# The first layer's FFN by seven block products as well, with its weight sums formed by POOL inside the stage

## The chip, the cores and the metric

The kernel runs on one core of a Trainium2 chip. The metric is the time of one execution on the device in microseconds (us); of the kernel before, three runs gave a median of 1687.15 us (1685.29 to 1689.51). The five engines of the core work beside each other: TensorE (PE) multiplies matrices, VectorE (DVE), ScalarE (ACT) and GpSimd (POOL) work on elements, SyncE (SP) starts the transfers (DMA). Each engine takes its instructions from its own queue in order and waits on semaphores for the others.

## The reference

Two layers over 512 latent tokens and 256 context tokens with 1024 features. Each layer mixes tokens by four groups of heads, and then applies a gated FFN with 2816 hidden features; shifts, scales and gates of each come from a conditioning vector by a matrix `w_mod`:

```python
def swiglu(h, w_in_, w_out_):
    gate, up = jnp.split(h @ w_in_, 2, axis=-1)
    return (jax.nn.silu(gate) * up) @ w_out_
...
    sh_a, sc_a, g_a, sh_f, sc_f, g_f = jnp.split((jax.nn.silu(c) @ w_mod + b_mod)[:, None, :], 6, axis=-1)
...
    x = x + g_a * rms_norm(mix_x @ w_out, norm_g[1])
    x = x + g_f * rms_norm(swiglu(modulate(rms_norm(x, norm_g[2]), sh_f, sc_f), w_ffn_in, w_ffn_out), norm_g[3])
```

`modulate(h, shift, scale)` is `h * (1 + scale) + shift`. All is float32. The output is the latent tokens after both layers.

## The kernel before

**Arithmetic.** Activations lie with features on the 128 partitions and tokens along the free axis. A float32 product is made of three matmuls: `split` (line 411) takes an operand apart into a rounded high part by ACT (`wh`, line 416) and the rest by DVE or POOL (`wl`, line 417), and `mac3` (line 489, matmuls on lines 491 to 493) multiplies high by high, high by low and low by high.

**FFN, plain.** The hidden features are 22 tiles of 128. For each, `ffn` loads two weight units of 512 KB (gate and up) into a ring of raw tiles `wr`, splits them, multiplies 8 blocks of features for each of gate and up, and gates. So a plain tile is 2 x 8 x 3 = 48 matmuls of 512 columns. Tiles are taken in chunks (`fcx`: 0 to 7, 8 to 14, 15 to 21), and behind each chunk the down product adds its hidden tiles to eight outputs `y`. The first three tiles and, of the last chunk, six of the eight outputs are done for the first 256 tokens and then for the second 256 (`halved`), so that the norm of one half runs beside matmuls of the other: behind the first half `ends` and `residual` norm it, and `then` starts the next layer's norm.

**FFN by seven block products.** Layer 1 uses `ffn_seven` and `strassen_pair`. Gate and up of one tile, the two halves of the features and the two halves of the tokens form a 2 by 2 block product, done by seven block products in place of eight; each is 4 x 3 = 12 matmuls of 256 columns, 84 per tile. It needs sums of blocks of the activations (`strassen_rhs`, once, `sx` and `st` tiles) and of the weights (`form_sums`, four 128 x 512 operations per tile). The first chunk's tiles stay plain, while these are formed. The weights' sums are either formed at the tile's turn, two operations by POOL and two by DVE (`sad`), or beforehand: `weight_sums` queues a task per tile that loads the two units, forms the sums by POOL alone (line 1566) and stores them, 1 MB, in DRAM (`ws`); the tile then loads them.

**Where the tasks run.** `tick` is called whenever a weight unit is fetched, and adds a rate to a counter; at 1 it takes one task off a queue. There are two queues: `bg` holds the tasks of the modulation (`mods_sums`: 32 tasks for layer 1, each one load of 512 KB and two multiply-adds by DVE into `macc`, lines 696 and 698; the totals go through PE on line 704 and DVE on line 708 to `mod`), and `bg2` the weights' sums. During layer 0's FFN `bg` runs at 0.2 per tick, and what is left is done by `flush` in `then`, at the boundary between the layers; `bg2` makes the sums of layer 1's nine even tiles 4 to 20 at 0.17 per tick.

**Order.** The program text gives priorities (`urgent` marks the norm chains as early); a scheduler with a time model then fixes each engine's queue before the run. Rings decide when buffers come free: raw weights `wr` for units, `wq` for the down weights of chunks, PSUM tiles `mm` and `mx`.

## Time and profile before

| | |
|---|---|
| median of three runs | 1687.15 us |
| profiled execution | 1681.38 us, span 1679.6 us |
| PE busy | 1596.8 us, 95% of the span |
| DVE, ACT, POOL busy | 1062.5, 792.8, 761.4 us |
| mean DMA rate | 146 GB/s |
| layer 0's FFN | about 640 to 1050 us of the span |
| boundary to layer 1 | about 1015 to 1060 us |
| layer 1's mixer | about 1053 to 1306 us |
| layer 1's FFN | about 1306 to 1680 us |

A time of the profile is counted from the start of the span. A busy engine is not an engine that works at its peak: matmuls overlap, so their pace is read from their starts and not from their durations. PEclk is the clock that TensorE was granted, where 1.00 is 2.4 GHz and 0.50 is 1.2 GHz. Idle time of an engine is listed with what ended it; for an engine that nothing waits for it costs nothing.

### The profile page before, as it was taken

The page shows a single profiled execution, that of the slowest core. Times are in us where ns is not written, and L with a number is a line of the kernel's source. Part 1 is how long each engine was busy: PE and PEld are TensorE (multiplying, and loading weights), DVE is VectorE, ACT ScalarE, POOL GpSimd, SP SyncE. Part 2 cuts the span into 40 slices and gives each one's busy share as a digit, 9 for nine tenths or more (in the row PEclk, how much of TensorE's full clock was granted, in tenths as well). Part 3 has the DMA queues.
Part 4 walks back from the last instruction along what each step waited for, and adds up shares of the span by engine and source line. Part 5 has one row for each costly group of instructions (what it writes and reads, how often), then busy time and mean ns, then how long its engine had stood idle before and what let it go on. Part 6 is the DMA issues. An engine that isn't in the chain of part 4 may idle for free.

```text
span 1679.6 us, 29082 instructions
## 1 busy us (share of the span) xinstructions
PE 1596.8 (95%) x10616; PEld 1395.7 (83%) x10616; DVE 1062.5 (63%) x2312; ACT 792.8 (47%) x1782; POOL 761.4 (45%) x797
## 2 busy tenths in 40 slices
PE   6999998998999998999999997999699999999997
PEld 2976877887899897888888887999569989999996
DVE  4887676648785668532343478658774866665664
ACT  3665356654445555332332333565374545555451
POOL 2431235554466565444335324332424665564653
PEclk8999998999999999999999998999799999999998
DMA  9854563354475323445545676131031224444441
GB/s 325 271 190 160 179 201 101 123 176 142 126 247 176 117 80 124 153 155 199 180 158 171 209 249 225 40 96 64 26 93 59 95 88 132 133 138 131 126 127 58
DMA packets 94734, 245.37 MB, mean 146 GB/s; under 512 B 12032, under 2 KB 21120, under 8 KB 94592
## 3 DMA queue, kind: packets, MB, share of 16 engines
q1 hardware_dynamic: 94592, 243.52, 44.2%
q8 instruction: 83, 1.36, 0.3%
q14 instruction: 59, 0.48, 0.1%
HBM read 227.76 MB, written 15.73 MB: 145 GB/s over the span
## 4 chain that ended last, share of the span: by engine, by line
PE 64%; DVE 7%; issue 1%; DMA 1%; POOL 1%; ACT 1%; DVEq 0%; POOLq 0%; SPq 0%; ACTq 0%
PE mm L491 16%; PE mm L493 15%; PE mm L492 15%; PE mx L493 2%; PE mx L491 2%; PE mx L492 2%; PE mm L508 1%; PE mm L513 1%; PE mm L514 1%; PE mm L515 1%; PE mm L509 1%; DVE wl L417 1%; PE mm L520 1%; PE mx L1420 1%; PE mx L1168 1%
## 5 line engine op out<-in xcount | busy, mean ns | idle before, releaser
L417 POOL TENSOR_TENSOR wl<-wr,wh 128x512 fp32r<-128x512 f32 (+2 forms) x268 | 358.9, 1344 | 428.1 <-ACT wh L416 390.5
L416 ACT ACTIVATE wh<-wr 128x512 fp32r<-128x512 f32 (+3 forms) x548 | 334.9, 619 | 459.3 <-PE mm L492 340.0
L417 DVE TENSOR_TENSOR wl<-wr,wh 128x512 fp32r<-128x512 f32 (+3 forms) x280 | 220.5, 790 | 155.1 <-ACT wh L416 149.7
L491 PE MATMUL mm<-hfh_m,wh 128*128 128x512 f32 (+1 forms) x320 | 124.6, 389 | 0.0
L493 PE MATMUL mm<-hfh_m,wl 128*128 128x512 f32 (+1 forms) x320 | 124.3, 388 | 0.0
L492 PE MATMUL mm<-hfl_m,wh 128*128 128x512 f32 (+1 forms) x320 | 123.9, 387 | 0.0
L492 PE MATMUL mm<-hfl_c,wh 128*128 128x256 f32 x352 | 100.3, 285 | 0.6 <-POOL hfl_c L603 0.6
L491 PE MATMUL mm<-hfh_c,wh 128*128 128x256 f32 x352 | 100.6, 287 | 0.0
L493 PE MATMUL mm<-hfh_c,wl 128*128 128x256 f32 x352 | 99.4, 283 | 0.0
L491 PEld LDWEIGHTS mm<-hfh_c,wh 128*128 128x128 f32 x352 | 66.1, 188 | 6.6 <-issue 2.7
L493 PEld LDWEIGHTS mm<-hfh_m,wl 128*128 128x128 f32 x320 | 60.1, 188 | 13.5
L492 PEld LDWEIGHTS mm<-hfl_m,wh 128*128 128x128 f32 x320 | 60.1, 188 | 13.2
L491 PEld LDWEIGHTS mm<-hfh_m,wh 128*128 128x128 f32 x320 | 60.1, 188 | 12.9
L492 PEld LDWEIGHTS mm<-hfl_c,wh 128*128 128x128 f32 x352 | 66.4, 189 | 2.4 <-issue 1.0
L493 PEld LDWEIGHTS mm<-hfh_c,wl 128*128 128x128 f32 x352 | 66.4, 189 | 0.8 <-issue 0.4
L492 PE MATMUL mm<-gl_m,wh 128*128 128x512 f32 x152 | 59.7, 394 | 0.0
L493 PE MATMUL mm<-gh_m,wl 128*128 128x512 f32 x152 | 59.7, 394 | 0.0
L491 PE MATMUL mm<-gh_m,wh 128*128 128x512 f32 x152 | 59.6, 394 | 0.0
L698 DVE SCALAR_TENSOR_TENSOR macc_m<-wr,cs,macc_m 128x512 f32<-128x512 f32 x56 | 45.8, 836 | 18.0 <-DMA wr<-in_wmod_dram 17.6
L1566 POOL TENSOR_TENSOR wr<-wr,wr 128x512 f32<-128x512 f32 x36 | 52.8, 1479 | 1.1
L491 PE MATMUL mx<-gh_m,wh 128*128 128x512 f32 x128 | 50.9, 399 | 1.4 <-ACT wh L416 1.4
L493 PE MATMUL mx<-gh_m,wl 128*128 128x512 f32 x128 | 51.2, 400 | 1.0 <-POOL wl L417 0.6
(721 smaller groups left out, 5329.2 us busy)
## 6 DMA issues: line engine op xcount, KB each, us to landing
wr<-in_wfi_dram SPq DMA_DIRECT2D x141, 512.0 KB, 3.6
wr<-in_wmod_dram SPq DMA_DIRECT2D x80, 512.0 KB, 4.4
wr<-in_wT_dram SPq DMA_DIRECT2D x42, 512.0 KB, 4.4
wr<-in_wo_dram SPq DMA_DIRECT2D x24, 512.0 KB, 4.2
wr<-in_wfo_dram SPq DMA_DIRECT2D x24, 512.0 KB, 4.0
wr<-ws SPq DMA_DIRECT2D x18, 512.0 KB, 3.9
wm_m<-in_wmod_dram SPq DMA_DIRECT2D x32, 256.0 KB, 5.3
wr<-in_wfo_dram SPq DMA_DIRECT2D x16, 448.0 KB, 3.9
```

What stands on the lines that cost most here:

```text
L416: nc.scalar.activation(hi, src, AF.Copy)
L417: (eng or nc.vector).tensor_tensor(out=lo, in0=src, in1=hi.bitcast(F32), op=ALU.subtract)
L491: nc.tensor.matmul(out, lh, rh, start=first, stop=False, skip_group_check=more)
L492: nc.tensor.matmul(out, lh, rl, start=False, stop=False, skip_group_check=more)
L493: nc.tensor.matmul(out, ll, rh, start=False, stop=last, skip_group_check=more)
L508: nc.tensor.matmul(out, w.h[w0 + i], ah, start=f, stop=False)
L509: nc.tensor.matmul(out, w.l[w0 + i], ah, start=False, stop=False)
L513: nc.tensor.matmul(out[:, c], w.h[w0 + i], ah[:, c], start=f and q == 0, stop=False)
L514: nc.tensor.matmul(out[:, c], w.h[w0 + i], al[:, c], start=False, stop=False)
L515: nc.tensor.matmul(out[:, c], w.l[w0 + i], ah[:, c], start=False, stop=z and q == 1)
L698: nc.vector.scalar_tensor_tensor(out=t, in0=w, scalar=self.cs[:, k, s:s + 1], in1=t, op0=ALU.mult, op1=ALU.add)
L1566: tt = lambda i, o, a, b, op=ALU.subtract: self.e(engines[i]).tensor_tensor(out=o, in0=a, in1=b, op=op)
```

## The change

Layer 0's FFN is done by `ffn_seven` too. Its first chunk are six plain tiles (0 to 5), then come four chunks of four tiles by block products. Eight of its sixteen tiles (7, 9, ... 21) get their weights' sums from tasks that POOL works off during the stage itself, at 0.5 per tick; a task whose tile was already formed at its turn is skipped (`formed`). The modulation's tasks of layer 1 run at 0.5 per tick. Layer 1's nine sums tasks move to layer 1's mixer, at 0.3 per tick, with the rest at its end. The down weights of a first chunk of over five tiles come through `wr` and not through `wq`.

```diff
- 'strassen': (1,),
- 'fcs': ((0, 4), (4, 7), (7, 11), (11, 16), (16, 22)),
- 'sums0': tuple(range(4, 22)),
+ 'strassen': (0, 1),
+ 'fcs0': ((0, 6), (6, 10), (10, 14), (14, 18), (18, 22)),
+ 'fcs1': ((0, 4), (4, 7), (7, 11), (11, 16), (16, 22)),
+ 'sums0': tuple(range(7, 22, 2)),
...
- 'pre_l0': 0.35,
- 'pre_f0': 0.17,
+ 'pre_f0': 0.5,
...
-        self.bg2.extend(lambda j=j: task(j) for j in js)
+        self.bg2.extend(lambda j=j: (l, j) in self.formed or task(j) for j in js)
...
         else:
+            self.formed.add((l, j))
             second = self.raw_unit(self.I["wfi"][l, j, 1])
...
-            w = self.weights(*self.ffo(l, m, j0, j1), ring=None if end else self.wq)
+            w = self.weights(*self.ffo(l, m, j0, j1), ring=None if end or j1 - j0 > 5 else self.wq)
...
             self.mods_sums(1, (2, 4, 3, 5), pn, 1)
-            if 0 not in T["strassen"]:
-                self.queue_sums(1, "pre_f0")
+            self.bg_rate = T["rate2"]
+            self.queue_sums(0, "pre_f0")
 
         self.layer_end(0, X, p, pn, norm, proj, mix)
-        self.flush_sums()
...
-        if 0 in T["strassen"]:
-            self.queue_sums(1, "pre_l1")
+        self.queue_sums(1, "pre_l1")
...
-        ffn, chunks = (self.ffn_seven, T["fcs"]) if l in T["strassen"] else (self.ffn, T["fcx"])
+        ffn, chunks = (self.ffn_seven, T[f"fcs{l}"]) if l in T["strassen"] else (self.ffn, T["fcx"])
```

In the changed file lines behind 294 stand one further down, so line 417 is 418 there and line 1566 is 1567.

POOL's queue ahead of layer 0's FFN, where the second half of the tokens is normed. `sq_t` are the square sums, `rmsy` the power of the norm, `x_m` the latent tokens, `wt` and `wl` low parts of weights, `wr` raw weights and their sums. Before:

```order
L617 TENSOR_TENSOR x_m_7447<-x_m_7447,rs_t_8191 128x256
L417 TENSOR_TENSOR wl_8166<-wr_8159,wh_8165 128x512
L550 TENSOR_TENSOR sq_t_8201<-sq_t_8201,sq_t_8204 128x256
L617 TENSOR_TENSOR x_m_7449<-x_m_7449,rs_t_8196 128x256
L550 TENSOR_TENSOR sq_t_8201<-sq_t_8201,sq_t_8209 128x256
L417 TENSOR_TENSOR wt_m_8284<-wr_8281,wt_m_8283 128x512
L550 TENSOR_TENSOR sq_t_8201<-sq_t_8201,sq_t_8214 128x256
L525 TENSOR_TENSOR rmsy_8225<-rmsv_8224,mhalf 128x2
```

The same place now:

```order
L618 TENSOR_TENSOR x_m_7447<-x_m_7447,rs_t_8191 128x256
L418 TENSOR_TENSOR wt_m_8280<-wr_8277,wt_m_8279 128x512
L551 TENSOR_TENSOR sq_t_8201<-sq_t_8201,sq_t_8204 128x256
L618 TENSOR_TENSOR x_m_7449<-x_m_7449,rs_t_8196 128x256
L1567 TENSOR_TENSOR wr_8784<-wr_8782 128x512
L551 TENSOR_TENSOR sq_t_8201<-sq_t_8201,sq_t_8209 128x256
L1567 TENSOR_TENSOR wr_8782<-wr_8780,wr_8782 128x512
L1567 TENSOR_TENSOR wr_8784<-wr_8784,wr_8780 128x512
L551 TENSOR_TENSOR sq_t_8201<-sq_t_8201,sq_t_8214 128x256
L1567 TENSOR_TENSOR wr_8780<-wr_8780,wr_8784 128x512
L526 TENSOR_TENSOR rmsy_8225<-rmsv_8224,mhalf 128x2
```

The first task's four operations have come between the adds and the power.

POOL's queue early in layer 0's FFN, now, while the last plain tiles and the first chunk's down product run (`sx` and `st` belong to the activations' block sums):

```order
L418 TENSOR_TENSOR st3l_m_9211<-sx_m_9220,st3h_m_9210 128x512
L418 TENSOR_TENSOR wl_9265<-wr_9262,wh_9264 128x512
L1567 TENSOR_TENSOR wr_9322<-wr_9320,wr_9322 128x512
L1567 TENSOR_TENSOR wr_9324<-wr_9324,wr_9320 128x512
L1567 TENSOR_TENSOR wr_9320<-wr_9320,wr_9324 128x512
L418 TENSOR_TENSOR wl_9336<-wr_9333,wh_9335 128x512
L1567 TENSOR_TENSOR wr_9438<-wr_9436 128x512
L1567 TENSOR_TENSOR wr_9436<-wr_9434,wr_9436 128x512
L1567 TENSOR_TENSOR wr_9438<-wr_9438,wr_9434 128x512
L418 TENSOR_TENSOR wl_9384<-wr_9381,wh_9383 128x512
```

Before, the same queue held more splits between fewer sums:

```order
L417 TENSOR_TENSOR wl_8858<-wr_8855,wh_8857 128x512
L417 TENSOR_TENSOR wl_8929<-wr_8926,wh_8928 128x512
L417 TENSOR_TENSOR wl_8952<-wr_8949,wh_8951 128x512
L417 TENSOR_TENSOR wl_9018<-wr_9015,wh_9017 128x512
L1566 TENSOR_TENSOR wr_9219<-wr_9217 128x512
L1566 TENSOR_TENSOR wr_9217<-wr_9215,wr_9217 128x512
L1566 TENSOR_TENSOR wr_9219<-wr_9219,wr_9215 128x512
L417 TENSOR_TENSOR wl_9028<-wr_9025,wh_9027 128x512
```

Sums and splits of weights now alternate without a run of splits alone.

DVE's queue at the end of layer 0's FFN, around the first half's norm (`y_m` down product, `sq_m` square sums, `rmsv` the mean of squares). Before:

```order
L696 TENSOR_SCALAR macc_m_11526<-wr_11524,cs 128x512
L696 TENSOR_SCALAR macc_m_11549<-wr_11547,cs 128x512
L698 SCALAR_TENSOR_TENSOR macc_m_11526<-wr_11524,cs,macc_m_11526 128x512
L698 SCALAR_TENSOR_TENSOR macc_m_11549<-wr_11547,cs,macc_m_11549 128x512
L1477 TENSOR_TENSOR y_m_9173<-mm_11270,y_m_9173 128x256
L698 SCALAR_TENSOR_TENSOR macc_m_11526<-wr_11529,cs,macc_m_11526 128x512
L698 SCALAR_TENSOR_TENSOR macc_m_11549<-wr_11552,cs,macc_m_11549 128x512
L582 TENSOR_SCALAR rmsv_11428<-ms_11423 128x2
```

Now:

```order
L1478 TENSOR_TENSOR y_m_9257<-mm_13134,y_m_9257 128x256
L551 TENSOR_TENSOR sq_m_12946<-sq_m_12946,sq_e_13131 128x256
L1478 TENSOR_TENSOR y_m_9258<-mm_13150,y_m_9258 128x256
L551 TENSOR_TENSOR sq_m_12946<-sq_m_12946,sq_e_13164 128x256
L418 TENSOR_TENSOR wt_m_13366<-wr_13359,wt_m_13365 128x512
L583 TENSOR_SCALAR rmsv_13221<-ms_13216 128x2
```

The modulation's operations have gone from this place.

## Rows read from the trace of the kernel before

**Rows 1.** The page: its head, and the ending chain by engine

```profile
span 1679.6 us, 29082 instructions
...
PE 64%; DVE 7%; issue 1%; DMA 1%; POOL 1%; ACT 1%; DVEq 0%; POOLq 0%; SPq 0%; ACTq 0%
```

**Rows 2.** Windows: stretch, length, busy time (count) per engine, clock, DMA, GB/s

```profile
747.00:850.00 103.00, 103.00 (x451) 83.68 (x450) 32.00 (x44) 33.52 (x56) 41.03 (x31) 1.00 0.52 176
1400.00:1500.00 100.00, 100.00 (x723) 94.33 (x722) 62.92 (x95) 52.66 (x100) 54.62 (x41) 1.00 0.42 131
...
1318.00:1400.00 82.00, 78.38 (x572) 73.08 (x571) 56.95 (x79) 39.24 (x81) 52.28 (x40) 0.98 0.26 83
```

The columns are PE, PE's weight loads, DVE, ACT and POOL, then PEclk and the share of the DMA engines.

**Rows 3.** Timeline of PE: start, duration, instruction; plain tile, then block products

```profile
724.89 0.40 PE L491 MATMUL mm<-hfh_m,wh 128*128 128x512 f32 x1
...
732.99 0.40 PE L493 MATMUL mm<-hfh_m,wl 128*128 128x512 f32 x1
...
1409.43 0.29 PE L491 MATMUL mm<-hf11h_m,wh 128*128 128x256 f32 x1
...
1413.82 0.28 PE L493 MATMUL mm<-st3h_m,wl 128*128 128x256 f32 x1
```

**Rows 4.** Timeline of POOL at the norm ahead of layer 0's FFN

```profile
661.93 0.72 POOL L525 TENSOR_TENSOR rmsy<-rmsv,mhalf 128x2 f32<-128x2 f32 x1 [3.74 <-DVE rmsv L582]
```

**Rows 5.** PE's waits, 640 to 670: total, times, longest

```profile
PE mm L508 <- ACT hfh_m L598: 0.5, 1, 0.5
```

**Rows 6.** POOL by line and shape, 664 to 1015: busy, mean ns; idle before

```profile
L417 POOL TENSOR_TENSOR wl<-wr,wh 128x512 fp32r<-128x512 f32 x56 | 74.7, 1335 | 151.1 <-ACT wh L416 146.9 <-PE mm L492 4.2
L1566 POOL TENSOR_TENSOR wr<-wr,wr 128x512 f32<-128x512 f32 x27 | 38.7, 1448 | 0.6
L1566 POOL TENSOR_TENSOR wr<-wr 128x512 f32<-128x512 f32 x9 | 11.6, 1290 | 23.5 <-DVE wl L417 23.5
```

**Rows 7.** POOL by line and shape, 1318 to 1400

```profile
L1540 POOL TENSOR_TENSOR sx_m<-sx_m,sx_m 128x512 f32<-128x512 f32 x4 | 6.9, 1729 | 0.6 <-DVE sx_m L1540 0.6
...
L417 POOL TENSOR_TENSOR st3l_m<-sx_m,st3h_m 128x512 fp32r<-128x512 f32 x2 | 3.5, 1760 | 0.0
L417 POOL TENSOR_TENSOR st0l_m<-sx_m,st0h_m 128x512 fp32r<-128x512 f32 x2 | 3.2, 1612 | 0.0
L1540 POOL TENSOR_TENSOR sx_m<-hf01h_m,hf01l_m 128x512 f32<-128x512 f32 x2 | 3.0, 1522 | 2.4 <-issue 2.4
...
L1540 POOL TENSOR_TENSOR sx_m<-hf10h_m,hf10l_m 128x512 f32<-128x512 f32 x2 | 2.8, 1383 | 0.0
```

**Rows 8.** Windows: the densest DMA; the late part of layer 1's mixer

```profile
990.00:1000.00 10.00, 10.00 (x55) 8.55 (x54) 9.96 (x16) 1.19 (x2) 1.74 (x1) 1.00 0.97 351
...
1175.00:1235.00 60.00, 43.66 (x275) 33.17 (x275) 47.29 (x171) 28.73 (x92) 22.09 (x32) 0.80 0.06 18
```

**Rows 9.** DVE by line and shape, 747 to 850

```profile
L698 DVE SCALAR_TENSOR_TENSOR macc_m<-wr,cs,macc_m 128x512 f32<-128x512 f32 x7 | 5.9, 849 | 4.2 <-DMA wr<-in_wmod_dram 4.1
```

**Rows 10.** Timelines of DVE and of POOL in layer 1's FFN

```profile
1452.09 1.77 DVE L1566 TENSOR_TENSOR wr<-wr,wr 128x512 f32<-128x512 f32 x1
...
1456.01 1.42 DVE L1653 TENSOR_TENSOR fe_m<-fe_m,fd_m 128x256 f32<-128x256 f32 x1
...
1451.70 1.62 POOL L1566 TENSOR_TENSOR wr<-wr,wr 128x512 f32<-128x512 f32 x1
...
1455.86 1.30 POOL L417 TENSOR_TENSOR wl<-wr,wh 128x512 fp32r<-128x512 f32 x1 [1.11 <-ACT wh L416]
```

**Rows 11.** Windows at the boundary between the layers

```profile
1030.00:1040.00 10.00, 3.42 (x21) 3.13 (x20) 10.00 (x14) 4.96 (x13) 8.45 (x17) 0.81 0.32 97
1040.00:1050.00 10.00, 6.79 (x30) 6.54 (x30) 6.29 (x16) 2.89 (x6) 2.88 (x5) 0.50 0.90 325
1050.00:1060.00 10.00, 9.97 (x58) 9.45 (x58) 8.31 (x18) 5.12 (x13) 6.11 (x9) 0.67 0.19 70
```

**Rows 12.** PE's waits, 988 to 1060: total, times, longest

```profile
PE ms L704 <- DVE mod L708: 9.3, 3, 5.3
```

More of the change, by code (lines that the diff above doesn't have):

```diff
@@ L293, in __init__ @@
         self.sums = {}
+        self.formed = set()
         self.bg2 = deque()
@@ L1918, in run @@
         self.bg_rate = T["rate0"]
-        if 0 in T["strassen"]:
-            self.queue_sums(0, "pre_l0")
         def flush_ctx():
@@ L1980, in run @@
         self.ph = 5
-        if 0 in T["strassen"]:
-            self.queue_sums(1, "pre_l1")
+        self.queue_sums(1, "pre_l1")
         self.order(T["l1"], 1, X, C, hx, p, self.ring(T["r1"]), {})
```

## The prediction

> **What bounds the kernel now.** I read the page first [rows 1]: the profiled execution spans 1679.6 us, and TensorE (PE) alone makes up 64% of the chain that ended last. Every other engine's share there is single figures, so the reader should see a kernel that ends when TensorE has worked through its matmuls, plus the places where it waits. Then the windows by stage [rows 2]: in 747 to 850, inside the first layer's FFN, PE is busy 103.00 of 103 us, and in 1400 to 1500, the same stage of the second layer (already in seven block products), 100.00 of 100. In both, fewer matmul columns are time saved at once, as long as the other engines hand over operands in time. At the start of the second layer's block products (1318 to 1400) PE still gets 78.38 of 82. So the change is worth what it takes from PE, minus what four places lose: the norm ahead of the stage, the first 80 us of the stage, the boundary between the layers, and the second layer's mixer. The profiled execution took 1681.38 us, 5.8 below the median of 1687.15; the sum is made against the former and carried over to the median.
>
> **PE's work.** In [rows 3] 512-column matmuls start 0.2314 us apart (724.89 to 732.99, 35 steps) and 256-column ones 0.1186 us (1409.43 to 1413.82, 37 steps). Behind the halved first three tiles, before has 19 plain tiles of 48 matmuls (912), 402 of the down product at 512 columns (192 + 168 + 42), and 12 x 7 x 3 = 252 at 256: 1314 x 0.2314 + 252 x 0.1186 = 304.1 + 29.9 = 334.0 us. After has only 256-column ones: 3 plain tiles of 96 (288), 16 tiles of 7 x 12 = 84 (1344), and the down product 288 + 3 x 192 + 48 + 144 = 1056; 2688 x 0.1186 = 318.8 us. That is **-15.2 us**. It includes that a 512-column matmul cut in two costs 0.237 instead of 0.231, as the down product and plain tiles now are.
>
> **The norm ahead of the stage.** In POOL's queue four operations of the first sums task now stand between the adds of the second half's square sums and the small power (rmsy). Before, the power ran at 661.93, after 3.74 us in which POOL waited for DVE [rows 4], and PE waited 0.5 us for what follows from it [rows 5], so the chain has no slack. One add of one tile's halves at 1.290 and three of two tiles at 1.448 [rows 6] are 5.6 us. The last stands behind the final add, in the 3.74 us gap, and hides. The other three, 4.2 us, are in the way: **+4**. Bounds: 0, if the loads land early and POOL runs them while it waits for the adds' inputs, and 8, if it waits for their 512 KB loads as well.
>
> **The first 80 us of the stage.** From the fourth plain tile to the third product of tile 8, POOL's queue holds 28 sums operations (8 x 1.290 + 20 x 1.448 = 39.3 us), 7 block sums of the activations (4 x 1.729 + 2 x 1.522 + 1.383 = 11.3), 4 splits of those (2 x 1.760 + 2 x 1.612 = 6.7) and 19 weight splits (19 x 1.335 = 25.4), all by [rows 6, 7]: 82.7 us. PE's work beside them is 652 matmuls x 0.1186 = 77.3 and 2 us of small ones, 79.3. So POOL is 3.4 us short even if it never waits, and the weight splits that PE needs stand behind the sums. The nearest row is the second layer's start, 82 us with the same activation sums and two formed tiles but without tasks: there PE lost 82 - 78.38 = 3.6 us. Value: 3.6 + 3.4 = **+7**. Bounds: 0 (the splits run ahead of PE; before, POOL waits there for ACT, 151.1 us of 351 idle ahead of this line [rows 6]) and 27, worked out in the first rival. SP's queue is part of this: the two loads of 512 KB and the 1 MB store of each task, the saving of X and the modulation's loads add up to 32.5 MB in some 96 us of PE work, 339 GB/s, and the most that the trace shows is 351 [rows 8]. It just fits; what lands late falls into the same bound.
>
> Does DVE's added work matter? The second layer's stage has DVE 62.92 busy of 100 and PE full [rows 2]. Here come 32 modulation loads with two multiply-adds each: 64 x 0.849 [rows 9] = 54 us over the remaining stage of some 300, 18 per 100. Some 81 per 100 is under the limit: **0**, at most 8.
>
> One more thing in the trace speaks against the start [rows 10]. POOL's sum began at 1451.70 and ended at 1453.32; DVE's add of two SBUF operands began at 1452.09 and ended at 1453.86, 0.54 us after POOL. The same happens at 1455.86 to 1457.16 and 1456.01 to 1457.43. So each waits out the other rather than sharing. The Trainium skill (SBUF — State Buffer, "Who interferes with whom") states this as a lock: a DVE instruction with two SBUF inputs and a GpSimd one that reads SBUF exclude each other for the whole instruction. The trace agrees (a 0.4 us add takes 1.42), and by that rule alone the start would cost about 27 us instead of 7, so the sum would turn into a loss.
>
> **The boundary between the layers.** In 1030 to 1060 PE runs 21 + 30 + 58 = 109 matmuls [rows 11] where the full pace (10 us / 0.1186 = 84) would be 253; the difference is worth 17 us, at a granted clock of 0.50 in the middle (the lower of the two levels, 1.2 GHz, after PE had been busy 3.42 of the 10 us before). Of this 9.3 us is waiting for the flushed modulation (L704 on DVE's L708 [rows 12]). At a pace of a half all 32 tasks lie inside the stage: -9.3. But the cover shrinks: the down product's second half, which keeps PE busy while the first half is normed, falls from 6 x 7 x 3 = 126 matmuls to 6 x 4 x 3 = 72, so 54 x 0.1186 = +6.4; and of the sums tasks that now stand in POOL's queue among the square sums one operation of 1.4 us lies on the chain. That gives -1.5. With the chain shorter, PE is idle for less time and less runs at half clock; I take **-3**. Bounds: -9.3 (the cover wasn't needed) and +6 (all four operations of a task, 5.6 us, on the chain: -9.3 + 6.4 + 5.6, and as much as 3 more at the lower clock).
>
> **The second layer's mixer.** Layer 1's nine sums tasks now run there. From 1175 to 1235 it is bound by latency: PE 43.66 of 60, POOL 22.09 [rows 8]. Twenty operations (28.2 us) fit into POOL's free 37.9 us, but each can delay a small operation of the chain by up to 1.4 us. Five such chain operations of POOL stand behind a task: 0 to 7, value **+2**, since PE is full before 1175, and can't be delayed by more than what the later part holds.
>
> **Sum:** -15.2 + 4 + 7 + 0 - 3 + 2 = -5.2. The profiled execution goes to 1676.2, the median to 1682.0: **1682 us**, faster by 0.3%. A measurement of this kernel tells changes of over 0.3% (5 us) from none, so the forecast stands at that edge. Its own range is 1671 to 1692.
>
> **Rivals.** (1) *The start of the stage is bound by POOL and DVE in turn.* One mechanism: if the two can't work on SBUF operands at once, the 40 512-column and 8 256-column DVE operations of two SBUF operands in that stretch (splits, activation sums, modulation, formed sums) add their 0.54 and 0.27 us [rows 10] to POOL's 82.7: 106 us beside 79 of PE work, 27 instead of 7. It decides as soon as more than 12 of these 27 reach PE. Price: -5.2 + 20 = +15, **1702**, slower. For it: [rows 10]. [...] (2) *Everything at the start hides, and the boundary loses its wait.* 0 in place of 4 and 7, 0 in place of 2: -15.2 - 3 = -18, **1669**. For it: PE 100.00 of 100 in [rows 2] with POOL at 54.62 and DVE at 62.92; against it: POOL was never above 60 of 100 there. (3) *What the blocks give, the boundary and mixer take back.* Boundary +6, mixer +7: -15.2 + 4 + 7 + 6 + 7 = +9, **1696**. For it: the shorter cover, which is certain; against it: the waits of 9.3 us that go.
>
> **Chances.** Forecast 0.46, rival (1) 0.22, (2) 0.20, (3) 0.12. Faster by over 0.3%: all of (2) and 0.25 of the forecast, 0.45. Within 0.3%: 0.15 of the forecast and 0.03 of (3), 0.18. Slower: (1), 0.06 of the forecast and 0.09 of (3), 0.37. The range of 8 in 10 takes in (2) at the low end and (1) at the high: 1664 to 1704.
>
> **What would show it.** PE's matmuls behind the halved tiles should come to some 319 us when nothing waits. In the stage's first 80 us POOL should be busy over 90%, and PE's waits there (for POOL or DVE's weight splits, lines 417/418) some 7 us; over 20 is rival (1), under 2 is rival (2). L704's wait of 9.3 us at the boundary should be gone; if PE still does fewer than 150 matmuls in the 30 us behind the first half's norm, the cover is what counts, and (3) gains. The mixer from 1175 on (shifted) should take 60 to 64 us. The forecast is wrong if any one place loses over 12 us, or if DVE's operations in the steady stage keep PE waiting.

## The result, and the profile after

The change makes the kernel slower: 1760.28 us (median of four runs, 1755.73 to 1762.40) against 1686.22 us, a ratio of 1.0434 with a 95% interval of 1.0416 to 1.0451. I had forecast 1682 us, with a range of 1664 to 1704.

Three first matmuls divide the program into stretches: that of layer 0's FFN (`hf`), of layer 1's projections (`hx`) and of layer 1's FFN (`hf00` again). The timeline of PE on the line of the halved products, before (matmuls by operand, count, duration min/median/max in ns, first and last start):

```profile
L508 PE MATMUL mm<-hfh_m,wt_m x32: 277/281/388, 639.5 to 673.7; 128*128 128x256 f32 x32
L508 PE MATMUL mm<-hxh_m,wt_m x32: 276/280/582, 1052.9 to 1078.7; 128*128 128x256 f32 x32
L508 PE MATMUL mm<-hf00h_m,wt_m x16: 276/280/389, 1306.1 to 1310.2; 128*128 128x256 f32 x16
```

The same of after:

```profile
L509 PE MATMUL mm<-hf00h_m,wt_m x8: 278/282/386, 642.8 to 649.7; 128*128 128x256 f32 x8
L509 PE MATMUL mm<-hxh_m,wt_m x32: 276/280/583, 1105.7 to 1131.5; 128*128 128x256 f32 x32
L509 PE MATMUL mm<-hf00h_m,wt_m x16: 276/284/582, 1379.4 to 1385.2; 128*128 128x256 f32 x16
```

What lies ahead of layer 0's FFN became 3.3 us longer (642.8 - 639.5), layer 0's FFN with the boundary 49.5 us (462.9 against 413.4), layer 1's mixer with its output projection 20.5 us (273.7 against 253.2), and layer 1's FFN 1.0 us. That is 74.3 us, the difference of the spans.

The page of after, its head and the ending chain, which answer to [rows 1]:

```profile
span 1753.9 us, 31934 instructions
...
PE 63%; DVE 17%; DMA 9%; issue 5%; POOL 4%; ACT 2%; SPq 1%; DVEq 0%; POOLq 0%; ACTq 0%
```

DVE's share of the chain was 7% and DMA's 1%: the other engines now set the end in places where PE did. Windows of after, with the columns of [rows 2]; the first is the stretch that the prediction calls the first 80 us, the last the boundary of [rows 11]:

```profile
699.10:815.50 116.40, 101.22 (x748) 95.60 (x746) 82.68 (x90) 35.53 (x70) 94.19 (x77) 0.91 0.69 226
700.00:740.00 40.00, 40.00 (x319) 37.20 (x319) 34.37 (x41) 11.33 (x21) 37.07 (x37) 1.00 0.65 205
740.00:840.00 100.00, 81.11 (x578) 77.51 (x576) 64.31 (x69) 35.30 (x70) 71.57 (x50) 0.88 0.66 221
840.00:1040.00 200.00, 186.33 (x1555) 184.41 (x1555) 149.92 (x210) 85.91 (x160) 100.51 (x68) 1.00 0.52 169
1060.00:1105.70 45.70, 29.03 (x201) 27.58 (x199) 30.99 (x53) 16.27 (x37) 32.87 (x43) 0.79 0.71 240
```

At 0.1186 us per matmul, 740 to 840 holds 68.5 us of work and loses 31.5; 840 to 1040 loses 200 - 184.4 = 15.6; the boundary loses 45.7 - 23.8 = 21.9. (A matmul that reaches over the edge of a window is counted on both sides of it, so a loss read this way is good to some 0.3 us.) Before lost nothing in the plain stage, and 37.9 - 189 x 0.1186 = 15.5 at the boundary, as these two windows of it show:

```profile
697.00:1015.00 318.00, 318.00 (x1482) 261.12 (x1481) 138.32 (x201) 99.38 (x170) 121.12 (x95) 1.00 0.56 190
1015.00:1052.90 37.90, 28.08 (x189) 27.04 (x188) 32.51 (x61) 13.23 (x29) 19.93 (x32) 0.78 0.62 214
```

POOL's costliest groups of after from 740 to 840, which answer to [rows 6]:

```profile
L418 POOL TENSOR_TENSOR wl<-wr,wh 128x512 fp32r<-128x512 f32 x23 | 34.8, 1522 | 7.8 <-DMA wr<-in_wfi_dram 4.1 <-ACT wh L417 3.4
L1567 POOL TENSOR_TENSOR wr<-wr,wr 128x512 f32<-128x512 f32 x15 | 21.9, 1477 | 0.3
L1567 POOL TENSOR_TENSOR wr<-wr 128x512 f32<-128x512 f32 x7 | 9.8, 1403 | 19.0 <-DMA wr<-in_wfi_dram 11.1 <-DMA ws<-wr 7.9
```

POOL is busy for 72% here. The stretch that the prediction meant, from the fourth plain tile to the third product of tile 8, runs from 699.1 to 815.5: there POOL is busy 94.2 of 116.4 us, 81% and not over 90%, and PE loses 116.4 - 748 x 0.1186 = 27.7 us, all but 2 of them behind 739.5. From 740 to 840 POOL stands 19.0 us ahead of the first operation of a task, waiting for that task's load or for an earlier one's store, with weight splits behind it in its queue. DVE's multiply-adds in the same window, for [rows 9]:

```profile
L699 DVE SCALAR_TENSOR_TENSOR macc_m<-wr,cs,macc_m 128x512 f32<-128x512 f32 x14 | 21.3, 1524 | 7.4 <-DMA wr<-in_wmod_dram 7.2
```

They take 1524 ns in place of 849. PE's waits of after, 1060 to 1120, for [rows 12]:

```profile
PE ms L576 <- DVE sq_t L551: 11.6, 2, 11.4
```

The 9.3 us for the modulation are gone, as the change intended, and 11.6 us for the square sums of the next norm have come.

### The profile page after: what moved, and what is told of

It is laid out like the page before. It is cut to its first block, busy times and chain, and to the rows that moved or that the text cites. A ratio compares the mean times of both kernels' runs of the same rounds, so it can differ in the third digit from the quotient of the medians.

```text
span 1753.9 us, 31934 instructions
## 1 busy us (share of the span) xinstructions
PE 1618.4 (92%) x11738; PEld 1464.9 (84%) x11738; DVE 1203.1 (69%) x2436; ACT 836.5 (48%) x1886; POOL 905.3 (52%) x889
## 4 chain that ended last, share of the span: by engine, by line
PE 63%; DVE 17%; DMA 9%; issue 5%; POOL 4%; ACT 2%; SPq 1%; DVEq 0%; POOLq 0%; ACTq 0%
PE mm L492 14%; PE mm L493 14%; PE mm L494 13%; DMA wr<-in_wmod_dram 3%; DVE wl L418 3%; DVE macc_m L699 2%; POOL wr L1567 2%; PE mx L494 2%; PE ms L656 2%; PE mx L492 2%; PE mx L1169 2%; PE mx L493 2%; DMA wr<-in_wfi_dram 1%; DMA ws<-wr 1%; PE mx L1163 1%
## 5 line engine op out<-in xcount | busy, mean ns | idle before, releaser
L1567 POOL TENSOR_TENSOR wr<-wr,wr 128x512 f32<-128x512 f32 x68 | 99.3, 1471 | 1.5
L516 PE MATMUL mx<-gh_m,wl 128*128 128x256 f32 x288 | 83.5, 290 | 12.9 <-DVE wl L418 7.2
L514 PE MATMUL mx<-gh_m,wh 128*128 128x256 f32 x288 | 83.2, 289 | 3.8 <-ACT wh L417 3.2
L515 PE MATMUL mx<-gl_m,wh 128*128 128x256 f32 x288 | 82.2, 286 | 0.0
L1567 POOL TENSOR_TENSOR wr<-wr 128x512 f32<-128x512 f32 x34 | 45.3, 1333 | 55.0 <-DMA wr<-in_wfi_dram 33.7
L418 POOL TENSOR_TENSOR wl<-wq,wh 128x512 fp32r<-128x512 f32 (+1 forms) x32 | 46.0, 1439 | 53.4 <-ACT wh L417 49.6
L516 PEld LDWEIGHTS mx<-gh_m,wl 128*128 128x128 f32 x288 | 55.8, 194 | 14.4 <-DVE wl L418 8.0
L514 PEld LDWEIGHTS mx<-gh_m,wh 128*128 128x128 f32 x288 | 56.0, 194 | 4.1 <-ACT wh L417 3.4
L515 PEld LDWEIGHTS mx<-gl_m,wh 128*128 128x128 f32 x288 | 55.8, 194 | 0.0
L494 PE MATMUL mm<-hf10h_m,wl 128*128 128x256 f32 x180 | 51.6, 287 | 3.2 <-DVE wl L418 3.2
```

Source lines behind the costliest of these rows:

```text
L418: (eng or nc.vector).tensor_tensor(out=lo, in0=src, in1=hi.bitcast(F32), op=ALU.subtract)
L494: nc.tensor.matmul(out, ll, rh, start=False, stop=last, skip_group_check=more)
L514: nc.tensor.matmul(out[:, c], w.h[w0 + i], ah[:, c], start=f and q == 0, stop=False)
L515: nc.tensor.matmul(out[:, c], w.h[w0 + i], al[:, c], start=False, stop=False)
L516: nc.tensor.matmul(out[:, c], w.l[w0 + i], ah[:, c], start=False, stop=z and q == 1)
L1567: tt = lambda i, o, a, b, op=ALU.subtract: self.e(engines[i]).tensor_tensor(out=o, in0=a, in1=b, op=op)
```

## The experiments

All stretches below are read as above, in us: "start" is the time of layer 0's FFN's first matmul, layer 0's FFN includes the boundary. A profile is one execution, and that of before lay 5 us under its median, so a single difference of up to 5 us in a stretch says nothing. The queues are fixed anew for each edit, so each difference also holds whatever a new order does.

| run | start | layer 0's FFN | mixer | layer 1's FFN | span | timed, median |
|---|---|---|---|---|---|---|
| before | 639.5 | 413.4 | 253.2 | 373.5 | 1679.6 | 1686.22 |
| after | 642.8 | 462.9 | 273.7 | 374.5 | 1753.9 | 1760.28 |
| e1 no tasks in layer 0 | 639.8 | 447.0 | 272.9 | 372.2 | 1731.9 | 1734.60 |
| e2 tasks on DVE | 640.7 | 448.7 | 267.2 | 372.7 | 1729.3 | 1731.94 |
| e3 ring of 9 | 659.9 | 453.8 | 269.0 | 382.6 | 1765.3 | 1769.23 |
| e4 modulation at 0.2 | 641.2 | 464.1 | 278.7 | 374.1 | 1758.1 | 1756.68 |
| e5 no tasks in layer 1 | 641.5 | 455.9 | 260.0 | 375.7 | 1733.1 | 1733.88 |
| e6 last chunk of six | 641.5 | 460.8 | 271.7 | 372.7 | 1746.7 | 1748.46 |
| e8 modulation without loads | 641.5 | 451.7 | 271.1 | 373.2 | 1737.5 | 1742.78 |
| e9 no tasks | 640.4 | 440.8 | 259.4 | 377.5 | 1718.1 | 1719.84 |
| e10 no tasks, no modulation | 639.9 | 410.6 | 260.1 | 376.8 | 1687.4 | 1690.28 |
| e11 modulation in mixer | 641.9 | 410.2 | 286.6 | 377.4 | 1716.1 | 1718.35 |
| e13 e9 without loads | 641.9 | 438.0 | 259.3 | 376.9 | 1716.1 | 1715.48 |
| e14 e9, one operand | 638.5 | 440.2 | 259.2 | 376.5 | 1714.4 | 1718.19 |
| e17 e13 and e14 | 639.5 | 426.7 | 260.4 | 377.2 | 1703.8 | 1704.74 |
| e7 before, modulation at 0.5 | 641.3 | 422.0 | 252.9 | 372.5 | 1688.7 | 1690.50 |
| e12 before, modulation late | 642.1 | 414.8 | 274.8 | 375.7 | 1707.4 | 1707.41 |
| e15 before, no tasks, 0.5 | 642.2 | 408.0 | 255.9 | 377.6 | 1683.7 | 1686.02 |
| e16 before, no tasks | 643.1 | 414.6 | 257.6 | 383.5 | 1698.8 | 1697.17 |
| e18 before, 5 tasks, 0.5 | 640.2 | 410.7 | 253.2 | 375.1 | 1679.2 | 1680.98 |

**The tasks of layer 0: e1 to e3.** Theory R: tasks hold the raw buffers, so PE's loads come late. Theory L: POOL and DVE take turns.

```diff
- 'sums0': tuple(range(7, 22, 2)),
+ 'sums0': (),
```

> After with no sums tasks in layer 0 (all 16 tiles of its block products form their sums at their own turn, two operations by POOL and two by DVE). Theory R (raw ring and transfers: a task holds three of the seven raw-weight buffers until its 1 MB store has left, so PE's own loads stand behind it in SP's queue): the 31 us that PE loses in the 100 us where the block products begin (about 740 to 840) falls under 8, the whole to 1725 to 1738 us. Theory L (POOL and DVE taking turns at SBUF operands): the same four operations per tile are still done by the same two engines, so the loss is spread over the stage and the whole stays within 1745 to 1765 us.

```diff
- 'sap': 'PPPP',
+ 'sap': 'VVVV',
```

> After with the tasks' four operations on DVE and not on POOL (both layers' tasks), with loads and stores as they were. Theory R: the loss where the block products begin stays between 25 and 40 us, the whole 1750 to 1780 us. Theory L, or POOL's queue alone: POOL is freed of some 40 us there and DVE needs 0.7 us per operation in place of 1.4, so the loss falls to 10 to 18 us and the whole to 1740 us or less.

```diff
- 'nctx': 26,
- 'wr': 7,
+ 'nctx': 22,
+ 'wr': 9,
```

> After with nine raw-weight buffers in place of seven (and four fewer slots of the context's arena, which makes the room). Theory R: the loss where the block products begin falls from 31 to 10 to 20 us, the whole to 1735 to 1750 us. Theory L: the same loss, 1755 to 1765 us.

e1's total, 1734.60, is what R said, but from 740 to 840 it still loses 13.7 us, not under 8. e2, with the same loads and buffers, gives 1731.94, against R; of the loss from 740 to 840 22.2 us are left, more than L's 10 to 18, and L's expectation took in POOL's queue alone, so e2 doesn't tell turn-taking from a full queue. e3 shortens the stage by 9.1 us and loses 19.1 in the same hundred us (757 to 857, as it starts 17 us later), as R said, but its smaller arena costs those 17 us ahead of the stage, so as a whole it is slower (1.0493, interval 1.0456 to 1.0529) and its total tells nothing. Neither theory holds alone. The tasks cost 15.9 us of the stage (after less e1; 15.1 by e5 less e9). Taking them off POOL's queue gives 14.2 us back, and two more buffers 9.1.

**The pace and the boundary: e4 to e6.**

```diff
-            self.bg_rate = T["rate2"]
+            self.bg_rate = T["rate1"]
```

> After with the modulation's tasks again at 0.2 per tick, the rest flushed at the boundary between the layers. If these tasks are what makes PE wait in the later stage (840 to 1060, 15.5 us lost to DVE's splits and sums), that loss falls to 5 us or less, and the boundary's loss rises from 22 us to 30 or more: 1755 to 1765 us in all. If DVE's own block-product work is the cause, the later stage still loses 12 us or more and the whole is 1768 us or more.

```diff
- 'sums1': tuple(range(4, 22, 2)),
+ 'sums1': (),
```

> After without layer 1's nine sums tasks (its 18 tiles form their sums at their own turn). If the tasks are what makes the mixer longer, its 273.7 us (from layer 1's first projection to its first FFN matmul) fall back to 253 to 258, and layer 1's FFN (374.5 us) gains 0 to 10: 1742 to 1752 us in all. If the mixer is longer for another reason (what follows from the boundary, or another order), it stays above 266 and the whole is 1758 us or more.

```diff
- 'fcs0': ((0, 6), (6, 10), (10, 14), (14, 18), (18, 22)),
+ 'fcs0': ((0, 6), (6, 10), (10, 13), (13, 16), (16, 22)),
```

> After with the last chunk of layer 0's FFN six tiles wide (four, three and three before it), so that the down product's second half, beside which the first half is normed, has 108 matmuls and not 72. Theory C (the shorter cover makes the boundary dearer): the boundary's loss of some 22 us falls by 4 to 5, the whole to 1750 to 1757 us. If the norm chain itself became slower (POOL's operations between its adds), it changes by less than 2 us.

e4 changes nothing as a whole: from 840 to 1040 it loses 10.7 us in place of 15.6, between what its two readings said, and the flush at the boundary takes that back. e5 gave more than any single edit but e2: 13.7 us of the mixer and 7.0 of layer 0's stretch, where the first tasks had come into the norm at the boundary; layer 1's FFN pays 1.2 us for forming all sums itself. It came out 8 us under its range. e6's whole is 12 us down, under its range too, and layer 0's stretch gives only 2.1 of it. But the boundary itself must be read by itself. Each kernel's last 45.7 us ahead of layer 1's first projection, of after (above), e6, e5 and e7 (the kernel before with the modulation at 0.5, below):

```profile
1056.60:1102.30 45.70, 31.74 (x244) 30.97 (x242) 28.74 (x49) 15.43 (x35) 29.21 (x40) 0.85 0.53 180
1051.70:1097.40 45.70, 34.53 (x262) 33.15 (x260) 33.47 (x60) 20.94 (x44) 21.78 (x35) 0.87 0.57 190
1017.60:1063.30 45.70, 40.78 (x307) 39.39 (x305) 26.78 (x50) 16.62 (x37) 20.79 (x34) 0.91 0.30 96
```

By their matmuls these lose 16.8, 14.6 and 9.3 us, where after loses 21.9 and before 15.3. So e6's longer cover gives 5.1 us at the boundary, as theory C said, and 3.0 are lost again earlier in the stage. The other runs fall into the same groups: with layer 1's tasks 20.6 to 22.8 (e1, e3, e8), without them 14.0 to 16.2 (e9, e10, e13, e14, e17), and with the long cover of the kernel before and the modulation at 0.5 they lose 8.9 (e15, e18). (e11 and e12, whose modulation begins at the boundary, lose 20.8 and 20.0.) Within a group the runs lie 2 us apart, so these steps stand clear: the modulation's move is worth 6 us, the shorter cover costs about 6, and layer 1's tasks some 6.5.

The chain of after in the mixer shows the tasks that e5 removes, among the mixer's own powers (`bys`):

```profile
1198.47 5.22 DMA ws<-wr
1203.71 4.43 DMA wr<-in_wfi_dram
1208.33 1.27 POOL wr L1567
1209.67 1.71 POOL wr L1567 x2
...
1212.47 1.03 POOL bys L526
```

**The modulation beside block products: e8 to e11.** In e8 the multiply-adds read a table (`self.cos`) in place of loaded weights; e10 is e9 with that edit and keeps one operation in eight.

```diff
-            raw = self.wr.tile([P, UNIT], F32, tag="wr", name=self.name("wr"))
...
-                w = raw[:, (k - k0) * 512:(k - k0) * 512 + 512]
+                w = self.cos[:, 0:512]
```

> After with the modulation's multiply-adds of layer 1 reading a table that lies in SBUF in place of loaded weights (the layer's modulation is then not the reference's): the same operations on DVE, without loads, raw buffers and waits for them. Theory Q (DVE stands in its queue waiting for the modulation's loads, with weight splits behind): the 13 us lost from 840 to 1040 fall to 5 or less, and the start of the block products gains 5 to 15: 1730 to 1745 us. Theory W (DVE's work itself is too much beside POOL's): the loss from 840 on stays above 9, the whole above 1750 us.

e9 joins the edits of e1 and e5.

> After with no sums tasks in either layer. If the two effects seen apart add (16 us of layer 0's stage, and 7 of the stage and 14 of the mixer), the stage is 437 to 447 us, the mixer 258 to 262, the whole 1710 to 1722 us. If both hang on the same cause, the whole stays above 1725 us.

```diff
- 'sums0': tuple(range(7, 22, 2)),
- 'sums1': tuple(range(4, 22, 2)),
+ 'sums0': (),
+ 'sums1': (),
...
-                    else:
-                        nc.vector.scalar_tensor_tensor(out=t, in0=w, scalar=self.cs[:, k, s:s + 1], in1=t, op0=ALU.mult, op1=ALU.add)
```

> As e9, and of the modulation's 32 tasks of layer 1 only the first operation of each group of eight, on a table in SBUF, is left (its values aren't the reference's, the rest of the modulation isn't computed). Theory W (DVE and POOL have room in the block-product stage for the stage's own work, as in layer 1, and what is too much is the work laid in beside it): the stage falls to 400 to 412 us (413.4 less 15 of PE's work and the boundary's waits of 9, plus the shorter cover and the start), the whole to 1672 to 1690 us. Theory S (layer 0's stage is slower for itself: its start, X saved and reloaded, fine pieces): it stays above 425 us.

```diff
-            self.bg_rate = T["rate2"]
+            self.bg_rate = 0.0
...
+        if l == 1:
+            self.flush()
...
-                self.flush()
+                self.bg_rate = T["rate0"]
```

> As e9, with all 32 modulation tasks of layer 1 taken out of layer 0's FFN and out of the boundary and run in layer 1's mixer at 0.8 per tick, flushed before its output projection; a whole kernel. If the stage is as in e10, 400 to 412 us, and the mixer, bound by latency, takes 5 to 20 us for the 54 us of DVE's work, the whole is 1678 to 1700 us. If DVE's work in the mixer lies on its chain, the mixer is 290 us or more and the whole above 1705.

e8's whole lies in Q's range (1742.78), and the loss that it leaves from 840 to 1040 (10.5 us) in W's: it doesn't tell them apart. In e9 the two effects add. e10 decides: with nothing laid beside it the stage runs at PE's pace behind 820 (from 740 to 840 it still loses 5.0 us). Its whole, 1690.28, is just over its range. Two windows of e10, then the same of e9:

```profile
860.00:880.00 20.00, 20.00 (x171) 20.00 (x170) 15.10 (x22) 9.66 (x18) 12.00 (x8) 1.00 0.31 101
...
940.00:960.00 20.00, 20.00 (x172) 20.00 (x171) 16.63 (x24) 9.99 (x18) 12.14 (x9) 1.00 0.37 119
```

```profile
860.00:880.00 20.00, 14.83 (x106) 14.62 (x105) 15.23 (x19) 6.18 (x13) 10.32 (x8) 0.83 0.34 119
...
940.00:960.00 20.00, 14.89 (x112) 14.68 (x110) 15.62 (x20) 6.17 (x12) 9.87 (x8) 0.83 0.41 136
```

So the modulation costs 440.8 - 410.6 = 30.2 us in this stage (29.6 by the medians of the whole), with DVE at 15 to 17 of 20 either way. Theory W holds against S as to the place of the loss. Yet even e10, with most of the modulation not computed, isn't faster than before (1690.28 against 1687.03): the 2.8 us that its stage gains are less than the 10 that its mixer and FFN of layer 1 take above before's. e11 moves the modulation into the mixer: the stage is that of e10, and the mixer pays 27.2 us (286.6 against 259.4), more than the 5 to 20 that I gave it.

How such a hole comes about, in DVE's timeline of e9 (start, duration, instruction, idle before):

```profile
781.67 0.75 DVE L699 SCALAR_TENSOR_TENSOR macc_m<-wr,cs,macc_m 128x512 f32<-128x512 f32 x1 [2.76 <-DMA wr<-in_wmod_dram]
782.34 0.42 DVE L1644 TENSOR_TENSOR fd_m<-mm,fd_m 128x256 f32<-128x256 f32 x1
...
783.67 3.46 DVE L418 TENSOR_TENSOR wl<-wr,wh 128x512 fp32r<-128x512 f32 x2
787.04 3.47 DVE L1567 TENSOR_TENSOR wr<-wr,wr 128x512 f32<-128x512 f32 x2
790.43 0.41 DVE L1654 TENSOR_TENSOR fe_m<-mm,fe_m 128x256 f32<-128x256 f32 x1
```

And in POOL's:

```profile
783.50 1.39 POOL L1567 TENSOR_TENSOR wr<-wr 128x512 f32<-128x512 f32 x1 [6.85 <-DVE macc_m L699]
784.97 1.61 POOL L1567 TENSOR_TENSOR wr<-wr,wr 128x512 f32<-128x512 f32 x1
786.54 3.43 POOL L418 TENSOR_TENSOR wl<-wr,wh 128x512 fp32r<-128x512 f32 x2
```

What PE and ACT wait for beside it:

```profile
782.81 0.39 PE L492 MATMUL mm<-st3h_m,wh 128*128 128x256 f32 x1 [2.19 <-DVE fd_m L1644]
790.88 0.63 ACT L417 ACTIVATE gh_m<-fe_m 128x512 fp32r<-128x512 f32 x1 [5.05 <-DVE fe_m L1654]
792.35 0.39 PE L492 MATMUL mm<-st1h_m,wh 128*128 128x256 f32 x1 [2.55 <-ACT fe_m L1636]
```

DVE waits 2.76 us for a load of the modulation; POOL waits 6.85 us for the raw buffer that the multiply-add still holds. Behind the multiply-add DVE adds up a product of PE's (`fd_m`), and PE waits 2.19 us for that. Then DVE and POOL both have a backlog of two-operand operations and take turns: DVE's four take 6.9 us, 1.73 each, where such a split takes 0.68 alone (e9, at 792.15). Behind these four stands DVE's next read of a product (`fe_m`, 790.43); ACT waits 5.05 us for it, and PE 2.55 for ACT. So in this hole PE lacks results that are read late, not weights. It has a granted clock of 0.83 from 780 to 790. Later in the stage it is weights: from 840 to 1030 12.1 of the 16.2 us that PE waits are for DVE's splits of the down weights (`mx` on L516).

**What of the modulation costs: e13, e14, e17.** e13 is e9 with e8's edit; e14 is e9 with multiplications in place of multiply-adds; e17 is both.

```diff
-                        nc.vector.scalar_tensor_tensor(out=t, in0=w, scalar=self.cs[:, k, s:s + 1], in1=t, op0=ALU.mult, op1=ALU.add)
+                        nc.vector.tensor_scalar(out=t, in0=w, scalar1=self.cs[:, k, s:s + 1], scalar2=1.0, op0=ALU.mult, op1=ALU.mult)
```

> As e9 (no sums tasks), with the modulation's multiply-adds reading a table that lies in SBUF in place of loaded weights (its values aren't the reference's): DVE's operations stay, loads and waits for them go. Of the 30 us that the modulation costs in the stage (440.8 against 410.6): by theory Q (DVE stands waiting for the loads with weight splits behind it) the stage falls under 420 us; by theory W (DVE's work, taking turns with POOL's, is what is too much) it stays above 430 us.

> As e9, with the modulation's multiply-adds done as multiplications of one tensor without the running total (its values aren't the reference's): loads and waits stay, the operation takes 0.49 us in place of 0.75 and has one SBUF operand in place of two. Theory Q: the stage stays above 430 us. Theory W without turn-taking: 56 x 0.26 = 15 us less of DVE's work, the stage loses about half of the 30 us, 422 to 430. Theory W with turn-taking (what hurts are two-operand operations that wait for POOL and that POOL waits for): under 422 us.

> As e13 and e14 together: no sums tasks, the modulation's operations on DVE with one SBUF operand (a table) and no loads (its values aren't the reference's). e13 (no waits, full work) and e14 (waits, less work) each left the stage at 438 to 440 us. Theory B (either of the two is enough to hold up the weight splits): with both gone the stage falls under 425 us. If what costs is only that 64 operations more stand in DVE's fixed order, whatever they are, it stays above 432 us.

Taking the loads and waits away gives 2.8 us of the 30.2, taking the second operand away 0.6, both too little to tell from nothing; both together give 14.1. So e13 refutes theory Q (waits alone). Whether e14 tests turn-taking is seen in DVE's groups: the multiply-adds of e9 (700 to 1040), and the multiplications of e14 and of e17 (697 to 1015):

```profile
L699 DVE SCALAR_TENSOR_TENSOR macc_m<-wr,cs,macc_m 128x512 f32<-128x512 f32 x53 | 58.7, 1107 | 18.8 <-DMA wr<-in_wmod_dram 18.6
L699 DVE TENSOR_SCALAR macc_m<-wr,cs 128x512 f32<-128x512 f32 x53 | 42.5, 802 | 33.5 <-DMA wr<-in_wmod_dram 32.9
L696 DVE TENSOR_SCALAR macc_m<-cos,cs 128x512 f32<-128x512 f32 x54 | 40.3, 746 | 0.7
```

And in the timelines of e17, a multiplication beside POOL and one without:

```profile
859.42 1.47 POOL L1564 TENSOR_TENSOR wr<-wr 128x512 f32<-128x512 f32 x1 [2.81 <-DVE wl L418]
859.77 1.40 DVE L696 TENSOR_SCALAR macc_m<-cos,cs 128x512 f32<-128x512 f32 x1
865.86 0.47 DVE L696 TENSOR_SCALAR macc_m<-cos,cs 128x512 f32<-128x512 f32 x1
```

e14 takes 16 us of DVE's work away and the stage stays, so W without turn-taking (work alone) is refuted. Turn-taking is not: I had expected that an operation with one SBUF operand takes 0.49 us wherever it stands, but these take 0.47 while POOL is idle, up to 1.6 beside POOL's operations, and 0.80 and 0.75 in the mean. e17's 426.7 lies between its theories: the waits and the work seem to replace each other as causes, and 16 us remain with multiplications that wait for no load but still take turns with POOL. Which of their length, their place in the order or the turn-taking makes these 16 stays open.

**Parts of the change on the kernel before: e7, e12, e15, e16, e18.**

```diff
             self.mods_sums(1, (2, 4, 3, 5), pn, 1)
+            self.bg_rate = T["rate2"]
```

> Before with only the modulation's pace raised to a half in layer 0's plain FFN, nothing else of the change. If DVE's multiply-adds hide beside plain tiles (PE full at DVE 32 of 103) and the boundary loses its 9.3 us of waits, the whole falls by 6 to 12 us against before. If the waiting of DVE for the modulation's loads holds up weight splits there too, PE loses in the stage what the boundary gains: within 4 us of before, or slower.

e12 has e11's flush in layer 1 and rate 0.8 there, and leaves 0.2 in the stage.

> Before with the 20 tasks that are left at the boundary run in layer 1's mixer at 0.8 per tick in place of being flushed. If the boundary's 9.3 us of waits and part of its half clock go, and the first 120 us of the mixer (PE full) hide the tasks, the whole falls by 5 to 12 us against before. If DVE's work delays the mixer's chain, it gains nothing or is slower.

e15 is e7 with `sums1` empty, e16 before with it empty, e18 e7 with `tuple(range(4, 22, 4))`.

> Before with the modulation's pace at a half as in e7 and layer 1's sums tasks left out (its tiles form their sums at their own turn); a whole kernel. If e7's loss came from DVE's waits for the modulation's loads (74.9 us idle, 17.6 in before), and these from the raw buffers that the tasks hold, the stage falls from e7's 422 to 398 to 406 us, layer 1's FFN takes up to 3 more, the whole 1672 to 1682 us, faster than before. If the pace alone costs (DVE's place in the order), it stays within 5 us of e7's 1690.

> Before with layer 1's sums tasks left out alone, the modulation's pace as it was. PE is full in layer 0's plain stage, so nothing is won there: within 4 us of before, and layer 1's FFN 0 to 3 us longer. It tells what of e15 is due to the pace.

> Before with the modulation's pace at a half and five sums tasks (tiles 4, 8, 12, 16, 20) in place of nine; a whole kernel. The raw buffers should be held less than in e7 (stage 422 us) and layer 1's FFN should keep more of its tasks' gain than in e15 (377.6 us against 373.5): a stage of 406 to 412 us, layer 1's FFN 373 to 376, the whole 1678 to 1685 us. If any task in that stage brings e7's waits back, 1688 us or more.

The pace alone is slightly slower even in the plain stage (e7: 1.0033, 1.0018 to 1.0047): the boundary gains 6.0 us, and the stage ahead of it loses 14.6, where DVE stands 74.9 us waiting for the modulation's loads. DVE's group of e7 from 697 to 1015:

```profile
L698 DVE SCALAR_TENSOR_TENSOR macc_m<-wr,cs,macc_m 128x512 f32<-128x512 f32 x54 | 47.2, 874 | 75.7 <-DMA wr<-in_wmod_dram 74.9
```

Of e18, with five tasks in place of nine:

```profile
L698 DVE SCALAR_TENSOR_TENSOR macc_m<-wr,cs,macc_m 128x512 f32<-128x512 f32 x54 | 45.4, 842 | 55.8 <-DMA wr<-in_wmod_dram 54.8
```

And of e15, with none:

```profile
L698 DVE SCALAR_TENSOR_TENSOR macc_m<-wr,cs,macc_m 128x512 f32<-128x512 f32 x55 | 44.0, 800 | 27.7 <-DMA wr<-in_wmod_dram 26.6
```

Fewer tasks, fewer waits, as expected from the raw buffers. e15's stage is 14 us shorter than e7's, 2 us over its forecast, but without tasks layer 1's FFN and mixer take 7 us more than before's, and the whole is the same as before (0.9997, 0.9988 to 1.0006), short of its forecast. Against e16 e15 is 11 us faster (1697.17 against 1686.02), but only 6.6 of it lie in the stage where the pace was changed; the rest lies in layer 1, where it wasn't. That e16 itself is 10 us slower than before, with 383.5 in layer 1's FFN, I had not expected, and its cause stays open. e18 lies in its forecast and keeps most of both sides: 1680.98 us, 0.9969 of before (0.9959 to 0.9979), the one version that beats both kernels. Five tasks at the old pace were not run, so how its gain divides between the pace and the number of tasks is not shown. e12 shows again what the mixer charges for DVE's work: 21.6 us, for a boundary that didn't get shorter.

## Why the prediction was wrong

- **PE's work (-15.2).** Right. In e10 PE does 171 and 172 matmuls in 20 us, its full pace, and the trace holds the work that was summed: 1314 matmuls of 512 columns and 736 others in before's stretch, 3173 others in e10's, which at the paces of [rows 3] are 391.3 and 376.3 us. That e10's stretch is nevertheless only 2.8 us shorter is time beside this work: 34.3 us in e10, 22.1 in before. The 12 us between lie up to 720 (13.5 against 6.3) and from 740 to 840 (5.0 against nothing), while from 1000 on the two lose the same (15.8 and 15.3). The 5.0 are near the 3.6 that the prediction took from layer 1's start. For the 7 us up to 720 it had no term; a wait for DVE's `ft_m` of 5.0 us in place of 3.4 and one of 1.3 for ACT's `av_c` are a part, and the rest stays open.
- **The norm ahead (+4).** About right. Its place is inside the stretch: counted from the stretch's start, POOL's small power ran after 22.4 us in before, 28.8 in after and 23.3 in e1, without these tasks, and PE's first matmul on the second half came after 27.3, 31.8 and 28.2 us. So the task costs 3.6 to 5.5. That the start itself came 3.3 us later shows nothing: it lies between 638.5 and 643.1 in the other runs (e3 aside).
- **The first 80 us (+7, bounds 0 to 27).** Too small: 27.7 us in the stretch that was meant, of which the tasks are the larger part (they cost 15.9 of the stage by e1, some 4 of it at the norm). POOL's work there was summed a little low: the operations that I put at 82.7 us took 91, and 7 us of small ones (`kw_c`) weren't in the sum. But POOL also stood 17.3 us ahead of the tasks' first operations, mostly for loads and stores; I had taken these as landed, though POOL waits for them in order with splits behind. That the first rival's 27 fits is partly luck: DVE and POOL did take turns (multiply-adds of 1524 ns), but the waits for transfers were no part of its sum.
- **DVE's added work (0, at most 8).** This is the step that failed, with the largest price. I wrote "Some 81 per 100 is under the limit: 0". By e9 against e10 the modulation costs 30.2 us, with DVE busy 262.8 of 340 us in e9, 77 per 100. Adding busy shares was the error: an engine that works in order beside another with which it takes turns, both bursty, delays PE well below 100. Most of the rows for it were there ([rows 10]), and I used them for the stage's start only. What of the 30.2 is waiting, work or turn-taking is open, as told above.
- **The boundary (-3, bounds -9.3 to +6).** The 9.3 us of waits went, and the loss rose by 6.6 (21.9 against 15.3 in 45.7 us). The cover, +6.4, was right: about 6, by e6 and by e9 against e15. The wait gave 6 and not 9.3, as a wait for square sums of 4.6 us remains when it is gone (e7, e15). The tasks of layer 1 cost some 6.5, where I had put one operation of 1.4 on the chain.
- **The mixer (+2, bounds 0 to 7).** It took 20.5; the tasks are 13.7 of it by e5. I counted delays of single POOL operations; the chain shows tasks in a row, with store, load and operations one after another, ahead of the mixer's own. The other 7 stay in every run of the changed kernel without tasks (259.2 to 260.4 against 253.2), and I did not find their cause.
- **Rivals.** The first had the right side and a place that was part of it, at 1702 not 1760. None had several places losing at once: I gave them one after another, each with the others at their middle. The signs that I had named against the forecast both came: places that lose over 12 us, and DVE's operations in the steady stage that keep PE waiting.

By the runs, layer 0's stretch is -15.2 + 30.2 (modulation) + 15.5 (its tasks, mean of two) + 6.6 (layer 1's tasks at the boundary, mean of 7.0 and 6.2) + 12.4 (what e10 keeps) = 49.5. The last term is what remains, so the sum comes out by construction; its places are told under PE's work.

## What to carry to other kernels

A stage that is full on one engine hides work on the others only as long as their queues don't hold what that engine needs behind something that waits. When its matmuls become shorter, price the side work by the stretch without it (leave it out, as in e10), not by adding busy shares. Look for what the full engine waits for, too: here it was first results that were read late, then weights. And test a bundle's parts alone on the kernel before: of the versions that were run only one beat before, the raised pace with fewer tasks beside it (e18), by 0.3%. Block products with the modulation at its old pace and no tasks were not run.

## What the runs showed of the hardware

A DVE operation on two SBUF operands took 1.73 us, in place of 0.68, for as long as POOL ran such operations back to back (e9, 783.67 to 790.5); POOL's took 1.4 to 1.7 beside them. How the 1.7 comes about is seen in the trace of before:

```profile
1393.56 1.63 POOL L1566 TENSOR_TENSOR wr<-wr,wr 128x512 f32<-128x512 f32 x1
1393.96 1.78 DVE L1566 TENSOR_TENSOR wr<-wr,wr 128x512 f32<-128x512 f32 x1
1395.15 1.74 POOL L417 TENSOR_TENSOR wl<-wq,wh 128x512 fp32r<-128x512 f32 x1
```

DVE's operation ends 0.55 us behind POOL's, and POOL's next one 1.15 behind DVE's: 1.70 for one of each. The prediction had this as a delay of 0.54 us per operation; with a backlog on both sides DVE loses 1.05 each. The Trainium skill (SBUF — State Buffer, "Who interferes with whom") says that a DVE instruction with two SBUF inputs contends with a GpSimd instruction that reads SBUF, and that this contention is an exclusive lock; this trace agrees.

A DVE multiplication with one SBUF operand and a column of scalars was held in the same way: 0.47 us while POOL was idle, up to 1.6 in e14 and 1.5 in e17 beside POOL's operations.
